# Quarter-column products of a modulation, issued by fours in place of pairs

## The chip, the cores and the metric

The kernel runs on one core of one Trainium2 chip. The metric is the device time of one execution in microseconds; of several runs the median is given. The profile is one execution taken by the hardware profiler; its rows are given in microseconds from the start of its span.

## What is computed

The reference is two transformer blocks behind each other, in float32, over 1024 tokens of width 1024. The first block modulates its input by a vector `c`, projects it to four mixers (an mLSTM, a gated spatial unit, a convolution and an S5 scan), projects back and runs a gated feed-forward layer. The second block normalises, projects, and runs attention, a state-space mixer and a linear recurrence. The part that the change touches is the modulation, which is one vector times a matrix:

```
mod = silu(c) @ w_mod[l] + b_mod[l]            # (1, 1024) @ (1024, 6144)
sh1, sc1, g1, sh2, sc2, g2 = split(mod, 6)
h = x * (1 + sc1) + sh1                        # needed first
x = layer_norm(ALPHA * x + g1 * (y @ w_out), ...)
x = layer_norm(ALPHA * x + g2 * swiglu(x * (1 + sc2) + sh2, ...), ...)
```

The first two sixths, `sh1` and `sc1`, are computed at the start of the kernel. The other four are the late modulation: 4096 columns, in eight parts of 512.

## The kernel before

The kernel is written as some forty Python generators, one for each stream of work (gates, an mLSTM pair, S5 batches, convolution taps, the projection, the out projection and so on). `weave` hands out their steps: every `yield t, wait` says how many microseconds of TensorE work the step is planned to take and how long the stream then waits, and at each moment the first stream of a fixed list (`STREAMS`) that is ready goes on. The late modulation is three entries: `mod_gate(0)` with parts 0 and 1 (the gate g1), `mod_cols` with parts 2 to 5 (sh2 and sc2), which follow each other in one stream, and `mod_gate(1)` with parts 6 and 7 (the gate g2), which starts when the out projection has its first accumulators. The program is then scheduled once more (`schedule_with_timeline_sim=True`), so that the order on an engine can differ from that of the code.

One part, `mod_part(n)` at line 1288, takes a PSUM bank `pm` (pmod in the trace) and an accumulator `acc` (macc). The 1024 rows of its weights are eight blocks of 128 rows by 512 columns, loaded by SyncE's queue two at a time into tiles `wm2` of 512 KB (wm in the trace), line 1301. Every block is one product, issued by `quarter` at line 440:

```
def quarter(p, kk, lhs, x):
    r0 = 32 * (kk % 4)
    pe.matmul(p[r0:r0 + 32, :], lhs, x, start=kk < 4, stop=kk >= 4)
```

The stationary side is one column of silu(c) repeated 32 times, so block `kk` fills 32 columns of TensorE and 32 partitions of the bank, the quarter `kk % 4`; blocks 4 to 7 are added to the quarters of blocks 0 to 3. ScalarE copies the bank to `acc` with the scale 1/32 (line 1311), and one more matmul sums the 128 partitions (line 1317) or turns them into a column (line 1325).

The loop over `q` runs five times. In turn it loads tile `q`, waits a planned 3.0, issues the two quarters of tile `q - 1`, frees that tile and counts 0.8 of TensorE work. So two tiles are held at most, and one load is always ahead of the pair that is issued. `spare` takes a free buffer from the list `ub` or else `u`; a freed buffer goes to the end of its list, and a load into it waits for whatever last read it. SyncE's queue also carries the other weights: `wpart` (line 219) loads 256 KB into one of three `raw` tiles, which ScalarE and VectorE or GpSimd split into a high and a low half (whi, wlo) for the other products (pz, psv, po, pf in the trace).

Of the kernel before, what the change touches and what calls it, by code (L numbers as in the profile page):

```python
# [75 lines left out]
def tile_block(ctx: ExitStack, tc: tile.TileContext, A, out):  # L76
    nc = tc.nc
# [32 lines left out]
    def ub(name, shape=None, dt=F32):  # L110
        return C["ub"].get(name, shape, dt)

    def f512(name):
        return C["f"].get(name)

    def bank(name, shape=None):
        return C["ps"].get(name, shape)

    def spare(name, shape=None, dt=F32, order=("u", "ub")):
        while not any(C[k].free for k in order):  # L120
            yield 0.0, 0.7
        k = order[0] if C[order[0]].free else order[1]
        return C[k].get(name, shape or (128, 1024), dt)

    def free(*ts):
        for t in ts:
            if isinstance(t, (list, tuple)):
                free(*t)
            else:
                next(c for c in C.values() if t.name in c.used).put(t)  # L130

    def need(**n):
        while any(len(C[k].free) < x for k, x in n.items()):
            yield 0.0, 0.7
# [56 lines left out]
    def col(name, i=0, n=1):  # L191
        return cols[:, COL0[name] + i:COL0[name] + i + n]
# [12 lines left out]
    def half(x, hf):  # L205
        return x[:, hf * 512:(hf + 1) * 512]
# [211 lines left out]
    cs = const.tile([128, 23, 2], F32, name="cs")  # L418
# [7 lines left out]
    wms = {}  # L426
# [13 lines left out]
# [4 lines that stand above are left out]
    def mod_part(st):  # L444
        pmt = bank("pmt", (128, 8, 2))
        for n in range(2):
            pm = bank("pmod")
            for q in range(4):
                x = wms[st + 2 * n, q]
                for k in range(2):  # L450
                    quarter(pm, 2 * q + k, cs[:, 2 * q + k:2 * q + k + 16, :].rearrange("p a b -> p (a b)"), x[:, k, :])
                free(x)
                yield 0.8, 0.0
            row = f512("modrow")
            v.tensor_copy(row[:], pm[:])
            free(pm)
            for c in range(4):
                pe.matmul(pmt[:, 4 * n + c, :], row[:, c * 128:(c + 1) * 128], fold[:], start=True, stop=True)
            free(row)
            yield 0.8, 0.0  # L460
        a, b = slice(4 * st, 4 * st + 4), slice(8 + 4 * st, 12 + 4 * st)
        bias = lambda r: col("b_mod", r.start, 4).unsqueeze(2).to_broadcast([128, 4, 2])
        v.tensor_tensor(modA[:, a, :], pmt[:, 0:4, :], bias(a), op=ALU.add)
        v.scalar_tensor_tensor(modA[:, b, :], pmt[:, 4:8, :], 1.0, bias(b), op0=ALU.add, op1=ALU.add)
        free(pmt)
# [77 lines left out]
    def mod_rest():  # L543
        while "A" not in state:
            yield 0.0, 0.7
        mod_load(1)
        ctx_load(1)
        state.add("L")
        while "h0" not in state:
            yield 0.0, 0.7  # L550
        yield from mod_part(1)
        ctx_split(1)
        state.add("h1")
# [30 lines left out]
    def start():  # L584
        if SCF:
            load_scols()
        mod_load(0)
        ctx_load(0)
        if not SCF:
            load_scols()  # L590
        state.add("T")
        yield 0.0, 8.0
        yield from mod_part(0)
        ctx_split(0)
        state.add("h0")
# [692 lines left out]
    def mod_part(n):  # L1288
        which = {0: 0, 3: 1}.get(n // 2)
        if which is not None and n % 2 == 0:  # L1290
            yield from need(ub=1)
            grow_[which] = ub(f"g{which}b", (128, 1024))
            nc.gpsimd.dma_start(grow_[which][:], A["g_b"][which:which + 1, :].to_broadcast([128, 1024]))
        yield from need(f=1, ps=1)
        acc = f512("macc")
        pm = bank("pmod")
        wms = []
        for q in range(5):
            if q < 4:
                wm = yield from spare("wm2", (128, 2, 512), order=("ub", "u"))  # L1300
                nc.sync.dma_start(wm[:], A["w_mod"][4 + n, :, 2 * q:2 * q + 2, :])
                wms.append(wm)
                yield 0.0, 3.0
            if q:
                wm = wms[q - 1]
                for k in range(2):
                    kk = 2 * (q - 1) + k
                    quarter(pm, kk, cs[:, kk, 0:1].to_broadcast([128, 32]), wm[:, k, :])
                free(wm)
                yield 0.8, 0.0  # L1310
        s.activation(acc[:], pm[:], AF.Copy, scale=1.0 / 32)
        free(pm)
        yield 0.0, 3.0
        yield from need(ps=1)
        if which is not None:
            p = bank("pmr")
            pe.matmul(p[:], ones[:], acc[:], start=True, stop=True)
            x = half(grow_[which], n % 2)
            v.tensor_tensor(x, x, p[:], op=ALU.add)
            if n % 2:  # L1320
                done.add(f"g{which}")
        else:
            p = bank("pmb", (128, 4, 2))
            for j in range(4):
                pe.matmul(p[:, j, :], acc[:, j * 128:(j + 1) * 128], ones[:, 0:2], start=True, stop=True)
            o = 4 * (n - 2)
            v.tensor_tensor(modB[:, o:o + 4], p[:, :, 0], col("b_mod", 24 + o, 4), op=ALU.add)
        free(p, acc)
        yield 1.0, 0.0

    def mod_cols():
        for n in (2, 3, 4, 5):
            yield from mod_part(n)
        sc2 = small("sc2", [128, 8], bufs=1)
        v.tensor_scalar(sc2[:], modB[:, 8:16], 1.0, None, op0=ALU.add)
        v.tensor_tensor(ln1c[:, 0], col("ln1_w", 0, 8), sc2[:], op=ALU.mult)
        v.tensor_tensor(ln1c[:, 1], col("ln1_b", 0, 8), sc2[:], op=ALU.mult)
        v.tensor_tensor(ln1c[:, 1], ln1c[:, 1], modB[:, 0:8], op=ALU.add)
        done.add("mod")
# [1265 lines left out]
```

## Time and profile before

| | us |
|---|---|
| median of 3 runs | 2351.17 |
| lowest and highest of the runs | 2348.05, 2354.90 |
| the profiled execution, its time | 2351.56 |
| its span, first to last instruction | 2349.8 |
| TensorE busy in the span | 2209.2 |

The mean granted clock of TensorE over the span is 0.969 of full speed. Busy times count instructions that run, not those that wait. The ends of matrix multiplications are modelled, and those that follow each other overlap in the rows, so the duration of one is longer than the step to the next.

### The profile page before, as it was taken

To read this page: it belongs to the slowest core of one execution; us is meant where nothing else is said; L and a number is where in the kernel's file an instruction comes from. 1 tells how busy PE (TensorE), PEld (TensorE's weight loads), DVE (VectorE), ACT (ScalarE), POOL (GpSimd) and SP (SyncE) were. 2 spreads that over 40 slices of the span, in tenths; PEclk is the share of its full clock that TensorE was granted. 3 is DMA by queue.
4 is the path that set the end of the run, shared out by engine and by line. 5 is a ranking of instruction groups with operands and counts; after the bars stand their busy time and mean duration, and the time that the engine had idled before them with its cause. 6 is when DMAs were issued, how large, how long until landed. Compare 5 with 4: busy or idle time off the path is not lost.

```text
span 2349.8 us, 29871 instructions
## 1 busy us (share of the span) xinstructions
PE 2209.2 (94%) x11002; PEld 1743.7 (74%) x11002; DVE 1209.7 (51%) x2192; ACT 815.1 (35%) x1497; POOL 926.2 (39%) x806
## 2 busy tenths in 40 slices
PE   5998879797999999999999999999999999989998
PEld 2787657575778888888888877687777777767877
DVE  8689744886881202112121497666544667575011
ACT  2423222443352111111212244344422455575322
POOL 4465534837654123232323445122563331022543
PEclk7999989798999999999999999999999999999999
DMA  7311444444322111111111334243576443332564
GB/s 275 97 49 50 141 148 139 138 146 149 91 69 75 47 52 45 50 41 58 45 59 54 99 117 146 87 154 105 159 211 178 166 162 130 103 112 94 148 194 141
DMA packets 161971, 265.87 MB, mean 113 GB/s; under 512 B 16409, under 2 KB 67481, under 8 KB 161825
## 3 DMA queue, kind: packets, MB, share of 16 engines
q1 hardware_dynamic: 127440, 219.21, 29.6%
q10 hardware_dynamic: 32112, 36.99, 4.6%
q0 software_dynamic: 2272, 7.77, 0.9%
q8 instruction: 86, 1.41, 0.3%
q14 instruction: 61, 0.49, 0.1%
HBM read 210.12 MB, written 52.74 MB: 112 GB/s over the span
## 4 chain that ended last, share of the span: by engine, by line
PE 66%; DVE 15%; DMA 7%; issue 4%; ACT 4%; POOL 4%; SPq 1%; ACTq 0%; POOLq 0%; DVEq 0%
PE pf L253 6%; PE pf L251 6%; PE pf L255 6%; PE pz L251 6%; PE pz L253 6%; PE pz L255 6%; PE pg L238 3%; PE pg L239 3%; PE pg L240 3%; PE pfo L238 2%; PE pfo L239 2%; PE pfo L240 2%; PE pO L2359 2%; DVE cv L809 1%; POOL wlo L212 1%
## 5 line engine op out<-in xcount | busy, mean ns | idle before, releaser
L212 POOL TENSOR_TENSOR wlo<-raw,whi 128x512 fp32r<-128x512 f32 (+1 forms) x285 | 394.8, 1388 | 877.4 <-ACT whi L215 857.9
L215 ACT ACTIVATE whi<-raw 128x512 fp32r<-128x512 f32 (+1 forms) x432 | 267.4, 622 | 992.0 <-PE pf L253 293.4
L212 DVE TENSOR_TENSOR wlo<-raw,whi 128x512 fp32r<-128x512 f32 (+1 forms) x147 | 114.8, 781 | 364.6 <-ACT whi L215 364.1
L255 PE MATMUL pf<-h,wlo 128*128 128x512 f32 x704 | 230.8, 391 | 3.9 <-POOL wlo L212 2.3
L253 PE MATMUL pf<-h,whi 128*128 128x512 f32 x704 | 231.3, 391 | 0.0
L251 PE MATMUL pf<-h,whi 128*128 128x512 f32 x704 | 231.2, 391 | 0.1
L251 PE MATMUL pz<-u,whi 128*128 128x512 f32 x512 | 171.2, 404 | 1.4 <-DVE sptmp L1794 0.6
L253 PE MATMUL pz<-u,whi 128*128 128x512 f32 x512 | 166.2, 394 | 0.0
L255 PE MATMUL pz<-u,wlo 128*128 128x512 f32 x512 | 165.8, 395 | 0.0
L255 PEld LDWEIGHTS pf<-h,wlo 128*128 128x128 f32 x704 | 132.1, 188 | 34.7 <-POOL wlo L212 3.7
L251 PEld LDWEIGHTS pf<-h,whi 128*128 128x128 f32 x704 | 132.1, 188 | 29.3 <-ACT whi L215 0.5
L253 PEld LDWEIGHTS pf<-h,whi 128*128 128x128 f32 x704 | 132.1, 188 | 29.2
L239 PE MATMUL pg<-wlo,act 128*128 128x512 f32 x352 | 138.3, 393 | 0.7 <-DVE wlo L212 0.5
L238 PE MATMUL pg<-whi,act 128*128 128x512 f32 x352 | 137.2, 393 | 1.2 <-ACT whi L215 1.2
L240 PE MATMUL pg<-whi,act 128*128 128x512 f32 x352 | 137.0, 392 | 0.0
L251 PEld LDWEIGHTS pz<-u,whi 128*128 128x128 f32 x512 | 95.9, 189 | 26.0 <-issue 3.0
L253 PEld LDWEIGHTS pz<-u,whi 128*128 128x128 f32 x512 | 96.3, 188 | 22.9 <-issue 1.4
L255 PEld LDWEIGHTS pz<-u,wlo 128*128 128x128 f32 x512 | 96.3, 188 | 22.0 <-issue 0.7
L1579 DVE TENSOR_TENSOR x<-x,pg 128x512 f32<-128x512 f32 x80 | 53.7, 685 | 109.5 <-PE pg L240 109.3
L239 PE MATMUL pfo<-wlo,mix 128*128 128x512 f32 x256 | 100.7, 394 | 1.7 <-POOL wlo L212 1.7
L1552 DVE TENSOR_TENSOR a<-a,pf 128x512 f32<-128x512 f32 x44 | 28.6, 683 | 140.7 <-PE pf L255 140.7
L240 PE MATMUL pfo<-whi,mix 128*128 128x512 f32 x256 | 100.4, 393 | 0.0
(628 smaller groups left out, 4810.7 us busy)
## 6 DMA issues: line engine op xcount, KB each, us to landing
raw<-in_w_ffn_in_dram SPq DMA_DIRECT2D x108, 256.0 KB
wm<-in_w_mod_dram SPq DMA_DIRECT2D x48, 512.0 KB
raw<-in_w_out_dram SPq DMA_DIRECT2D x96, 256.0 KB
raw<-in_w2f_dram SPq DMA_DIRECT2D x66, 256.0 KB
raw<-in_w_ffn_out_dram SPq DMA_DIRECT2D x56, 256.0 KB
raw<-in_w2q_dram SPq DMA_DIRECT2D x48, 256.0 KB
raw<-in_w_in_dram SPq DMA_DIRECT2D x36, 256.0 KB
mraw<-y2d SPq DMA_DIRECT2D x32, 256.0 KB
```

Source lines behind the costliest of these rows:

```text
L212: (v if dve else g).tensor_tensor(lo, full, hi, op=ALU.subtract)
L215: s.activation(hi, full, AF.Copy)
L238: pe.matmul(p, lh, rh, start=start, stop=False)
L239: pe.matmul(p, lh, rl, start=False, stop=False)
L240: pe.matmul(p, ll, rh, start=False, stop=stop)
L251: pe.matmul(p, wh, xh[k], start=k == 0, stop=False)
L253: pe.matmul(p, wh, xl[k], start=False, stop=False)
L255: pe.matmul(p, wl, xh[k], start=False, stop=k == kt - 1)
L809: v.scalar_tensor_tensor(a3, *tap(k), a3, op0=ALU.mult, op1=ALU.add)
L1552: v.tensor_tensor(a_[:], a_[:], pair[1][hf][:], op=ALU.mult)
L1579: v.tensor_tensor(x, x, p[t][:], op=ALU.add)
L2359: pe.matmul(pO[64 * x:64 * x + 64, b, :], va[:, jb, 64 * x:64 * x + 64], PT[2 * hp + x, ib][:, jb, :], start=jb == 0, stop=jb == ib)
```

## The change

`mod_part` no longer pipelines loads against pairs. It runs two rounds. Each round takes two tiles, issues both loads, waits a planned 5.0, issues the four quarters of the two tiles behind each other, frees both tiles and counts 1.0 of TensorE work. The products, their operands and the loads are the same.

```
-        wms = []
-        for q in range(5):
-            if q < 4:
-                wm = yield from spare("wm2", (128, 2, 512), order=("ub", "u"))
-                nc.sync.dma_start(wm[:], A["w_mod"][4 + n, :, 2 * q:2 * q + 2, :])
-                wms.append(wm)
-                yield 0.0, 3.0
-            if q:
-                wm = wms[q - 1]
-                for k in range(2):
-                    kk = 2 * (q - 1) + k
-                    quarter(pm, kk, cs[:, kk, 0:1].to_broadcast([128, 32]), wm[:, k, :])
-                free(wm)
-                yield 0.8, 0.0
+        for q0 in (0, 2):
+            wms = []
+            for q in (q0, q0 + 1):
+                wms.append((yield from spare("wm2", (128, 2, 512), order=("ub", "u"))))
+                nc.sync.dma_start(wms[-1][:], A["w_mod"][4 + n, :, 2 * q:2 * q + 2, :])
+            yield 0.0, 5.0
+            for k in range(4):
+                kk = 2 * q0 + k
+                quarter(pm, kk, cs[:, kk, 0:1].to_broadcast([128, 32]), wms[k // 2][:, k % 2, :])
+            free(wms)
+            yield 1.0, 0.0
```

## Rows read from the trace of the kernel before

**Rows 1.** The head of the page: span, and busy time of each engine.
```profile
span 2349.8 us, 29871 instructions
PE 2209.2 (94%) x11002; PEld 1743.7 (74%) x11002; DVE 1209.7 (51%) x2192; ACT 815.1 (35%) x1497; POOL 926.2 (39%) x806
```

**Rows 2.** Busy by stage: length; PE, PEld, DVE, ACT, POOL; clock, DMA share, GB/s.
```profile
255.00:345.00 90.00, 69.79 (x398) 52.24 (x397) 43.21 (x86) 21.68 (x41) 41.73 (x46) 0.89 0.53 164
345.00:445.00 100.00, 93.50 (x535) 68.26 (x533) 64.11 (x132) 38.59 (x79) 61.74 (x59) 0.95 0.53 169
445.00:540.00 95.00, 79.20 (x456) 63.41 (x454) 78.09 (x207) 37.21 (x93) 52.58 (x73) 0.88 0.36 120
540.00:665.00 125.00, 111.32 (x458) 81.56 (x459) 97.49 (x149) 46.51 (x84) 72.94 (x54) 0.90 0.33 102
665.00:900.00 235.00, 231.17 (x1023) 188.76 (x1022) 65.35 (x91) 65.36 (x121) 90.48 (x63) 1.00 0.20 61
```

**Rows 3.** Waits of TensorE, 255 to 445 us: total us, times, longest.
```profile
PE pmod L442 <- DMA wm<-in_w_mod_dram: 7.0, 3, 4.2
```

**Rows 4.** TensorE's timeline, line 442: start, length, count, [idle before, what ended it].
```profile
287.37 1.06 PE L442 MATMUL pmod<-wm,cs 128*32 128x512 f32 x8
294.71 1.94 PE L442 MATMUL pmod<-wm,cs 128*32 128x512 f32 x8 [2.23 <-DMA wm<-in_w_mod_dram]
318.59 1.93 PE L442 MATMUL pmod<-wm,cs 128*32 128x512 f32 x8 [4.23 <-DMA wm<-in_w_mod_dram]
...
367.55 1.05 PE L442 MATMUL pmod<-wm,cs 128*32 128x512 f32 x4
372.72 1.05 PE L442 MATMUL pmod<-wm,cs 128*32 128x512 f32 x4
377.99 1.06 PE L442 MATMUL pmod<-wm,cs 128*32 128x512 f32 x8
...
560.19 1.92 PE L442 MATMUL pmod<-wm,cs 128*32 128x512 f32 x16
624.14 1.04 PE L442 MATMUL pmod<-wm,cs 128*32 128x512 f32 x2
627.14 1.04 PE L442 MATMUL pmod<-wm,cs 128*32 128x512 f32 x2
...
638.48 1.07 PE L442 MATMUL pmod<-wm,cs 128*32 128x512 f32 x8
```

**Rows 5.** Busy time in two short stretches, columns as in the second group.
```profile
287.30:288.50 1.20, 1.20 (x10) 0.27 (x10) 0.00 (x0) 0.74 (x2) 1.03 (x1) 1.00 0.27 101
294.70:296.70 2.00, 1.99 (x9) 0.33 (x9) 0.00 (x0) 0.00 (x0) 0.00 (x0) 0.50 0.13 36
```

**Rows 6.** The chain of waits that ended last: start, length, what.
```profile
288.46 6.21 DMA wm<-in_w_mod_dram
...
311.74 6.81 DMA wm<-in_w_mod_dram
...
328.12 4.67 DMA wm<-in_w_mod_dram
...
367.62 0.98 PE pmod L442 x4
368.61 0.67 PE pz L251 x2
369.28 0.47 PE pz L253 x2
...
378.06 0.99 PE pmod L442 x8
...
637.50 3.33 DVE x L1529
```

**Rows 7.** The timeline of SyncE's queue: two issues of line 1301.
```profile
368.65 0.33 SPq L1301 DMA_DIRECT2D wm<-in_w_mod_dram  x1
...
379.08 0.33 SPq L1301 DMA_DIRECT2D wm<-in_w_mod_dram  x1
```

## The prediction, made before the change was run

> **What bounds the kernel now.** I read the head of the page first: the span, and how much of it TensorE is busy [rows 1]. 2209.2 of 2349.8 us leave 140.6 us of idle TensorE in the whole kernel. So a change pays either by taking work off TensorE where TensorE is never idle, or by shortening some of that idle time.
>
> The second view is busy time by stage, cut where the late modulation runs [rows 2]. The reader is to take from it the difference of the second column from the first. From 255 to 345 us TensorE is idle for 20.2 us, from 345 to 445 for 6.5, from 445 to 540 for 15.8 and from 540 to 665 for 13.7, together 56.2. From 665 to 900 it is 231.17 of 235, and there the feed-forward block needs nothing more than the end of this work. Five of the eight parts of the modulation and most of its loads lie in 255 to 445 us; the last two parts lie in 545 to 665 us.
>
> The third view is who waited for whom on TensorE in 255 to 445 us [rows 3]: the products of the modulation waited for their weight tiles three times, 7.0 us in all. The fourth is the timeline of TensorE, with the rows of line 442 alone [rows 4]. Each quarter-column product is two matrix multiplications in the trace, so a pair is x4, four together are x8. The chain of waits [rows 6] says which of these rows set the end, and the timeline of the SyncE queue [rows 7] says when a load could be issued.
>
> **The change, part by part.** *What already runs as four.* A part of the modulation has eight quarters, in the code four pairs. The trace doesn't show 32 pairs. In part 0 both rows are x8 (287.37 and 294.71 [rows 4]), and so are the two rows of part 1 (318.59, and one at 327.03 like that at 287.37) and of part 2 (at 332.84 and 341.63, the same). Parts 3, 4 and 5 are each a pair, a pair and a four: the three rows from 367.55 to 377.99 stand for all three parts. Part 6 is one row of x16, two fours. Part 7 is two single quarters (624.14, 627.14), one more pair at 635.51, and a four at 638.48. So of the 16 fours that the new code writes, 12 run as fours already, and only four are in pieces: three in two pieces, one in three. That is five separate passes to be saved, not sixteen.
>
> *What a piece costs.* A pair takes 1.05 us, a four 1.06, a single quarter 1.04 [rows 4]. The time doesn't depend on how many run side by side. In the chain a pair occupies 0.98 and a four 0.99 [rows 6]. There is something behind it too: the first two full-width products after the pair at 367.62 take 0.67 where the next two take 0.47, 0.20 more [rows 6]. So a separate piece costs 0.98 + 0.20 = 1.18 us; the floor, without the 0.20, is 0.98. I take 1.18, since both rows stand in one place on the chain.
>
> The Trainium skill, page TensorEngine Tiling, section Tiling Modes, says that changing the tiling mode drains TensorE. The 0.20 us agrees with it, and by that page fewer groups also mean fewer drains; without it the sum below would be 0.6 us smaller.
>
> *Where the five pieces lie.* Three are in parts 3, 4 and 5, in 345 to 445 us, two of them (parts 3 and 4) in the stretch up to 407 us where the chain runs along TensorE without a gap; I count all three: 3 x 1.18 = 3.5 us. The other two are in part 7. There the chain has left TensorE for VectorE (from 637.50 [rows 6]), so those 2 x 1.18 = 2.4 us are hidden by VectorE work and I count nothing; with that cover gone they add 2.4 us of gain.
>
> *The loads.* All 32 loads of 512 KB on SyncE's queue remain, in the same order and with the same two tiles held. What changes is when they may go. Now a load goes out when the pair ahead of it has freed its tile: 368.65 follows the pair at 367.55, which ends at 368.60, and 379.08 follows the four that ends at 379.05 [rows 4, 7]. The tile is used two steps later, and a step was 372.72 - 367.55 = 5.17 us. After the change two loads go out together when a four has freed both tiles, and both are wanted one step later, which the code plans as 5.0 us. The planner's step of before, 3.0 + 0.8 = 3.8, took 5.17 us in this stretch, so 5.0 should take 5.0 x 5.17 / 3.8 = 6.8 us. What must fit in there: a pair of loads issued together at 328.12 landed 4.67 us later, a single one behind other traffic 6.21, one at the end of a burst of six 6.81 [rows 6]. So the lead, about 10 us now, shrinks to 6.8, just enough for the slowest of these rows. I count no new wait; its bounds are 0 and, with a lead of only the planned 5.0, 6.81 - 5.0 = 1.81 us for each group. Behind a waiting product stands all of TensorE's queue, in this stretch the projection (pz) and the mLSTM products, which need nothing from these tiles.
>
> The Trainium skill, DMA: Bandwidth & Descriptors, section Anatomy of one DMA, gives for the other issuing path 2.0 us and a term of bytes / 436e3; that would be an estimate of 4.4 us for 1 MB, near the 4.67, and by it the loads are always in time. The rows of 6.21 and 6.81 speak against relying on it.
>
> *The three waits of before* (7.0 us [rows 3]) are in parts 0, 1 and 2. Two of them brought the clock down: the four after a wait of 2.23 us took 1.94 us at a granted clock of 0.50 (1.2 GHz), where the four at 287.37 took 1.06 at 1.00 (2.4 GHz) [rows 4, 5]. That is 0.88 us more, twice. In these parts the products are fours already, and the loads that came late were held by tiles in use elsewhere, so I keep these waits: gain 0, with a bound of 7.0 + 2 x 0.88 = 8.8 us.
>
> *The planned times.* A part is planned as 4 x 0.8 + 1.0 of TensorE now and as 2 x 1.0 + 1.0 after, 1.2 less, 9.6 over eight parts; its planned waits are 4 x 3.0 against 2 x 5.0, 2.0 less. What the parts yield is not what the code after them waits for longest (the out projection also waits for the whole projection, the first normalisation for the out projection), so an earlier end of a part gains nothing by itself: 0. But the other streams are handed out in another order. The idle 56.2 us of [rows 2] are waits in such an order; I take no change and, as bounds, a fifth of it to either side, 11.2 us (an assumption of mine, not a row).
>
> *Sum.* 2351.56 us (the profiled execution, 1.76 more than its span and 0.4 above the median of the runs) - 3.5 = 2348.1. By the median, 2347.7. I say 2348.
>
> **The rivals.**
> *The loads come late.* Two loads at once, both wanted at once, one step ahead. For it: tiles are scarce, as each load waits for a pair [rows 7], and three waits exist already. Against it: the lead of 6.8. It decides when the lead falls below the landing time. If the six groups of parts 3 to 5 each wait 1.81 us and run at the lower clock, 6 x (1.81 + 0.88) = 16.1, less the 3.5 gained: 2351.6 + 12.6 = 2364. Slower.
>
> *The old waits go.* The halved number of steps lets the early loads go out in time. For it: the three waits came from tiles freed late, and fewer waits for tiles are on SyncE's queue. Gain 3.5 + 8.8 = 12.3: 2339. Against it: the tiles of the early parts belong to other streams, which the change doesn't touch.
>
> *Another order of the streams.* Either sign: 2348.1 - 11.2 = 2337, or 2348.1 + 11.2 = 2359. For it: the order on TensorE is already not that of the code (two quarters of one pair run 3 us apart at 624.14 and 627.14). Against it: 665 to 900 us is full of TensorE work whatever the order [rows 2].
>
> *The fours are not fours.* The scheduler parts them again, as it did that pair: gain 0, 2351.6.
>
> **How the numbers follow.** A measurement of this kernel tells 0.3%, 7 us, from no change. Chances: the forecast 0.34; fours that are not fours 0.08; old waits gone 0.19; loads late 0.15; another order 0.24, half to each side. So faster 0.19 + 0.12 = 0.31, same 0.34 + 0.08 = 0.42, slower 0.15 + 0.12 = 0.27. The likeliest case alone spans 2344 to 2355: the five pieces at 1.18 and one or two waits gone at the lower end, one or two late pairs of loads at the upper. Cases of both signs hold 0.58, so the range reaches to the ends of the rivals, 2337 to 2364.
>
> **What would show it.** Line 442 in x8 rows alone, 16 of them, each near 1.06 us (1.94 where the clock is down), and its busy time in 345 to 445 us down from nine pieces to six. The waits of those products for weight tiles near 7 us; over 15 us, and the first rival is right, below 2, and the second is. Loads in twos on SyncE's queue, landing in 4.7 to 6.8 us. TensorE's idle time in 255 to 665 us near 56 us: if it moved by 7 us or more without the waits on weight tiles, the order did it. Wrong would be the prediction if TensorE's busy time fell by 6 us or so while the span didn't follow, or if the span moved with line 442 unchanged.

## The result, and the profile after

The changed kernel takes 2374.4 us (median of 5 runs, 2371.1 to 2379.1), the kernel before 2351.2: a ratio of 1.010, 95% interval 1.0081 to 1.0119. It is slower by 1.0%, 23 us. The forecast was 2348 with a range of 2337 to 2364; the time lies 10 us above its end. The profiled execution took 2371.11 us. Lines of the kernel after the changed loop have moved up by three (L1317 of before is L1314).

The head of the page, to be set beside [rows 1]:

```profile
span 2369.4 us, 29876 instructions
PE 2218.7 (94%) x11002; PEld 1749.4 (74%) x11002; DVE 1206.1 (51%) x2192; ACT 815.3 (34%) x1498; POOL 924.3 (39%) x806
```

TensorE runs the same 11002 matrix multiplications. Busy time is up by 9.5 us and idle time (span less busy) from 140.6 to 150.7, 10.1 us. So about half of the 19.6 us of span is idle, and half is the same work done in more time.

Busy time by stage, at the same times as in [rows 2]:

```profile
255.00:345.00 90.00, 73.54 (x401) 57.36 (x400) 43.27 (x80) 24.91 (x49) 40.71 (x45) 0.85 0.38 118
345.00:445.00 100.00, 92.05 (x512) 64.64 (x510) 69.10 (x137) 38.23 (x74) 60.80 (x54) 0.97 0.61 195
445.00:540.00 95.00, 77.76 (x453) 62.43 (x452) 73.53 (x193) 34.66 (x90) 45.73 (x72) 0.87 0.28 94
540.00:665.00 125.00, 102.59 (x434) 75.00 (x433) 87.65 (x140) 43.00 (x80) 81.47 (x59) 0.92 0.37 122
665.00:900.00 235.00, 227.60 (x996) 184.94 (x995) 73.32 (x113) 64.97 (x120) 85.19 (x59) 0.99 0.20 62
```

The first four stages are now idle for 16.5, 8.0, 17.2 and 22.4 us, together 64.1 against 56.2. The stage that was to be full whatever the order, 665 to 900, is idle for 7.4 us in place of 3.8.

TensorE's timeline, the rows of line 442, which answer to [rows 4]:

```profile
288.06 1.06 PE L442 MATMUL pmod<-wm,cs 128*32 128x512 f32 x8
320.93 1.93 PE L442 MATMUL pmod<-wm,cs 128*32 128x512 f32 x8 [0.16 <-DMA wm<-in_w_mod_dram]
328.64 1.06 PE L442 MATMUL pmod<-wm,cs 128*32 128x512 f32 x8 [2.08 <-DMA wm<-in_w_mod_dram]
...
389.44 1.05 PE L442 MATMUL pmod<-wm,cs 128*32 128x512 f32 x4
391.55 1.05 PE L442 MATMUL pmod<-wm,cs 128*32 128x512 f32 x4
...
413.97 1.91 PE L442 MATMUL pmod<-wm,cs 128*32 128x512 f32 x12
422.79 1.05 PE L442 MATMUL pmod<-wm,cs 128*32 128x512 f32 x4
...
444.15 1.05 PE L442 MATMUL pmod<-wm,cs 128*32 128x512 f32 x4
445.55 1.05 PE L442 MATMUL pmod<-wm,cs 128*32 128x512 f32 x4
...
580.88 1.92 PE L442 MATMUL pmod<-wm,cs 128*32 128x512 f32 x16
```

Two things are to be seen. Although the code now hands out fours only, four of the 16 still come apart on TensorE (three are shown, at 389, at 414 with its last pair at 422, and at 444; one at 356 runs as one quarter and three). A pass is a group of at most four quarters side by side; there are 20 of them in place of 21. And part 0, whose two fours stood 7 us apart before (287.37 and 294.71 [rows 4]), now has 33 us between them, 288.06 and 320.93.

Line 442 alone, the sum over 255 to 700 us, first of the changed kernel and then of the kernel before (TensorE busy, its weight loads):

```profile
sum 445.00, PE 21.64 PEld 3.30; mean PE 7.21 PEld 1.10
```

```profile
sum 445.00, PE 23.76 PEld 3.35; mean PE 7.92 PEld 1.12
```

The products themselves became 2.1 us cheaper. TensorE's waits, 255 to 700 us:

```profile
PE phn L1023 <- POOL num L1016: 10.8, 2, 10.5
PE pkt L895 <- DVE modB L1324: 5.6, 1, 5.6
PE pf L255 <- DVE wlo L212: 3.7, 1, 3.7
...
PE pmod L442 <- DMA wm<-in_w_mod_dram: 2.2, 2, 2.1
```

The wait for weight tiles, 7.0 us in [rows 3], is 2.2 us. The long waits are of other streams: 10.5 us in front of the second half of the mLSTM output, 5.6 for a PSUM bank that a part of the modulation gives on. On GpSimd, a load of the gating unit's scale rows stood behind a product, since its tile had just been a weight tile of the modulation (timeline of GpSimd):

```profile
345.11 1.14 POOL L1061 DMA_DIRECT2D sw<-in_sgu_ln_dram  x2 [18.93 <-PE pmod L442]
```

Where the 19.6 us arise can be read from the first and last matmuls of each stage in TensorE's timeline. The out projection (po) starts 11.4 us later (509.4, 520.8), the feed-forward block (pf) 10.6 later (657.3, 667.9), its second product (pg) 14.7 later (777.3, 792.0); the last pf is 17.3 later and the end 19.6. So half is lost before 668 us, four us in the first feed-forward blocks, the rest behind it. That rest, 4.9 us, is within what single executions of one kernel differ by (2348.05 to 2354.90 before). And the later start of po is no price by itself: in E8 below po starts at 518.6, and the first pf comes at 656.7.

TensorE up to the first pf, and from there to the first pg, columns as in [rows 2]; first before, then after:

```profile
0.00:657.30 657.30, 554.93 (x2906) 424.47 (x2906) 485.21 (x899) 227.54 (x455) 350.20 (x364) 0.90 0.39 127
657.30:777.30 120.00, 116.09 (x514) 93.57 (x515) 50.43 (x75) 43.52 (x84) 57.32 (x38) 1.00 0.25 77
```

```profile
0.00:667.90 667.90, 559.92 (x2908) 427.55 (x2909) 485.48 (x895) 227.57 (x455) 352.37 (x364) 0.91 0.38 125
667.90:792.00 124.10, 116.70 (x514) 94.30 (x513) 50.54 (x78) 44.01 (x86) 56.69 (x38) 0.99 0.24 75
```

Up to the first pf TensorE has the same matrix multiplications to run (two more after the change, the sum over the partitions of part 7, pmr). It idles 5.6 us longer, and the same work takes 5.0 us more, though the mean granted clock is no lower. Why it takes more, these rows don't show.

### The profile page after: what moved, and what is told of

It reads as the page before. It is cut to its first block, busy times and chain, and to the rows that moved or that the text cites. A ratio compares the mean times of both kernels' runs of the same rounds, so it can differ in the third digit from the quotient of the medians.

```text
span 2369.4 us, 29876 instructions
## 1 busy us (share of the span) xinstructions
PE 2218.7 (94%) x11002; PEld 1749.4 (74%) x11002; DVE 1206.1 (51%) x2192; ACT 815.3 (34%) x1498; POOL 924.3 (39%) x806
## 4 chain that ended last, share of the span: by engine, by line
PE 66%; DVE 15%; DMA 7%; POOL 4%; issue 4%; ACT 3%; SPq 0%; ACTq 0%; DVEq 0%; POOLq 0%
PE pz L251 6%; PE pf L255 6%; PE pf L251 6%; PE pf L253 6%; PE pz L253 6%; PE pz L255 6%; PE pg L239 3%; PE pg L240 3%; PE pg L238 3%; DVE cv L809 2%; DMA raw<-in_w_out_dram 2%; POOL wlo L212 2%; PE pO L2356 2%; PE pfo L238 2%; PE pfo L239 2%
## 5 line engine op out<-in xcount | busy, mean ns | idle before, releaser
L253 PEld LDWEIGHTS pz<-u,whi 128*128 128x128 f32 x512 | 96.7, 189 | 22.8 <-issue 1.4
```

Source lines behind the costliest of these rows:

```text
L253: pe.matmul(p, wh, xl[k], start=False, stop=False)
```

## The experiments

Four theories. **A, the order:** the kernel's planner hands out work by the planned times of all streams and by free buffers; the new loop comes up at other moments and takes and frees its tiles two at a time, so other streams get other places, and that order is slower. **B, the products or their loads:** fours, or loads issued in twos, arrive late or hold up TensorE. **C, one wait:** GpSimd's 19 us behind the products delays the gating unit, and the rest follows. **D:** each new part costs a fixed few us.

Ratios are to the kernel before on the same chip, with 95% intervals.

**E1, fours at the old times.** The old loop with all its planned waits; only the products are put together.
```
-            if q:
+            if q in (1, 3):
                 (four products of tiles q - 1 and q)
-                free(wm)
+                free(wms[q - 1], wms[q])
+            if q:
                 yield 0.8, 0.0
```


> The quarters run by fours (blocks 0 to 3 once tiles 0 and 1 are loaded, blocks 4 to 7 once 2 and 3 are), but every planned time and hand-over of the loop of before stays, so that the other streams are handed out nearly as before; the second tile of a four has a planned lead of only 3.0. Theory A (the loss is the new order of the other streams, not the fours): within 7 us of before, 2344 to 2358. Theory B (both tiles of a four wanted at once is what costs, loads come late): at least as slow as the changed kernel, 2370 or more, with waits of line 442 on its tiles over 15 us. Theory C (one wait of GpSimd at the row load of the gated spatial unit): near before too if that 18.9 us wait is absent.

**E2, pairs with the new totals.** The old loop, `yield 0.0, 3.0` made 2.5 and `yield 0.8, 0.0` made 0.5.

> The pairs and the load one ahead of before stay; only the planned times change, 0.5 in place of 0.8 and 2.5 in place of 3.0, so that a part is planned with the totals of the changed kernel (3.0 of TensorE work, 10.0 of waits and the last 3.0). Theory A (order): the time moves by more than 7 us although the loop is the old one; to 2360 to 2385 if the smaller totals themselves give the bad order. Theory B (late loads for fours): 2351, within 7 us. Theory C: moves only if GpSimd's wait at the row load of the gated spatial unit appears (near 19 us).

**E3, the new loop with the old totals.** `yield 0.0, 5.0` made 6.0, `yield 1.0, 0.0` made 1.6.

> The changed kernel with a planned wait of 6.0 in place of 5.0 and 1.6 in place of 1.0 behind each four, so that a part is planned as long as before (15.2 us) with as much TensorE work (3.2). Theory A (order, through the planned totals): most of the 23 us comes back, 2345 to 2362. Theory B (late loads): one more microsecond of lead takes at most the 2.2 us that the products still wait for their tiles, so 2370 or more. Theory C: fast only if GpSimd's wait is gone.

**E4, the changed kernel without GpSimd's wait.**
```
-            nc.gpsimd.dma_start(lnwb[:, i, :], A["sgu_ln"]...
+            nc.sync.dma_start(lnwb[:, i, :], A["sgu_ln"]...
```


> The changed kernel, with the two row loads of the gated spatial unit issued by SyncE's queue in place of GpSimd's, so that GpSimd no longer stands 18.9 us behind the quarter products whose tile that unit takes over; SyncE waits there anyway. Theory C (this wait is the loss): 2351 to 2362, GpSimd's wait gone and TensorE's products of the gated spatial unit done by about 408 us in place of 424. Theory A (the order as a whole): little of it, 2368 to 2377. Theory B (late loads): no change, 2374.

Measured: E1 1.0008 (0.9996 to 1.0021), E2 1.0037 (1.0022 to 1.0051), E3 1.0093 (1.0070 to 1.0116), E4 1.0083 (1.0064 to 1.0102).

E1 answers B for the fours of the code: TensorE waits 1.1 us for their tiles, and they cost nothing measurable. On TensorE five of E1's fours are parted again, 22 passes in all, so E1 doesn't show what a saved pass is worth. E3 says that the smaller planned totals are not needed for the loss, E2 that pairs with the new totals lose a third of it. For E3, theory A had foretold 2345 to 2362 through the totals and B 2370 or more. It measured 2371.3, so that form of A falls; but TensorE waited only 2.0 us for weight tiles, so B's late loads are not the reason. In E4 the wait of 18.9 us is gone from GpSimd's list, but the long waits of TensorE stand as in the changed kernel:

```profile
PE phn L1023 <- POOL num L1016: 10.9, 2, 10.6
PE pu L1192 <- DVE modB L1324: 7.0, 1, 7.0
PE pf L255 <- DVE wlo L212: 3.7, 1, 3.7
```

So GpSimd's standing there accounts for at most some 0.2%, and the intervals of E4 and of the changed kernel overlap. The edit doesn't make the rows of the gating unit earlier, though. SyncE's queue (first line) issues them at 343.26 us, where GpSimd did at 345.11 in the changed kernel. The unit's products (second line) last until 421.2, 424.2 in the changed kernel and 407.6 before; theory C had foretold 408. So E4 doesn't test what late rows cost.

```profile
343.26 0.90 SPq L1061 DMA_DIRECT2D sw<-in_sgu_ln_dram  x2
L1084 PE MATMUL psg<-sw,vn x64: 272/273/324, 398.6 to 421.2; 128*64 128x128 f32 x64
```

**E5, E6, E7, the new loop in some parts alone**, the old one in the others: `if n in (0, 1)`, `(2, 3, 4, 5)`, `(6, 7)`.

> The new loop in parts 0 and 1 alone (the gate g1); parts 2 to 7 keep the old one. Theory A (the loss comes with the order of the other streams, set where the parts are handed out among the mLSTM, S5 and gated spatial streams): the loss belongs to one group of parts, most likely the first, since the gated spatial unit's wait and the second mLSTM pair come behind it: 2360 to 2376 here and GpSimd's wait at line 1061 present. Theory D (each part costs by itself, about 23 / 8 = 3 us, in the loads or the steps of the loop): 2351 + 6 = 2357.

> The new loop in parts 2 to 5 alone (shift and scale of the second half). Theory A: within 7 us of before (2344 to 2358) if the first group makes the loss, 2365 or more if this one does; not in between by four parts' worth. Theory D: 2351 + 12 = 2363.

> The new loop in parts 6 and 7 alone (the gate g2), which run when the out projection does. Theory A: within 7 us of before, 2344 to 2358, the mLSTM's second pair as early as before (its last transposes near 560 us). Theory D: 2351 + 6 = 2357.

**E8, another order without the change.** The kernel before, with the planned wait of an S5 batch `yield 0.0, 4.0` made 5.0.

> A control: the kernel before with one planned wait of another stream moved by one microsecond (5.0 in place of 4.0 in an S5 batch, behind its two products on GpSimd); no instruction is added, removed or changed. If the time of this kernel hangs on the order alone (theory A), such a step too should move it by several us, to either side: anywhere in 2344 to 2372. If only the loop of the modulation matters (theories B and D), 2351 within 3.

Measured: E5 1.0052 (1.0036 to 1.0068), E6 1.0032 (1.0021 to 1.0043), E7 1.0020 (1.0011 to 1.0030), E8 0.9991 (0.9978 to 1.0004). Per part that is 6.1, 1.9 and 2.4 us (ratio less 1, times 2351, by parts), so D, a fixed cost, falls. The three add up to 1.04%, near the 1.0% of the whole; E17 below shows that this sum is not to be trusted. Theory A, as it was written down for these runs, did not hold either: it put the loss in one group of parts and E6 not in between, where it lies. It also had E8 move by several us. E8's order did change (po starts 9.2 us later), so E8 shows that not every change of order costs.

In E7 TensorE's course is that of before up to the first pf (658.5 against 657.3 us). The time is lost in the first feed-forward blocks: first pf to first pg takes 126.4 us, before 120.0. The waits of TensorE there, first of E7 from 655 to 800 us, then of the kernel before from 657 to 800:

```profile
PE pf L255 <- DVE wlo L212: 5.1, 2, 3.6
PE pf L255 <- POOL wlo L212: 2.1, 1, 2.1
```

```profile
PE pf L255 <- POOL wlo L212: 2.3, 1, 2.3
PE pf L255 <- DVE wlo L212: 1.5, 1, 1.5
```

The changed kernel has 5.3 and 2.1 in the same two waits. From the first pf to the first pg in E7:

```profile
658.50:784.90 126.40, 119.17 (x514) 96.06 (x513) 50.55 (x78) 44.11 (x86) 55.95 (x38) 0.96 0.23 73
```

So the 6.4 us are 3.3 of idle time (7.2 in place of 3.9) and 3.1 for the same 514 matrix multiplications, at a mean granted clock of 0.96 in place of 1.00.

VectorE splits the weights and the inputs that TensorE waits for. In the first normalisation it also scales two rows and, with them, the residual. The second row is scaled at 615.71 us in E7 and at 634.30 before, since the last parts are done earlier.

**E9, E7 with the scaling held back.**
```
         yield from after("ffa")
+        yield 0.0, 13.0
```


> The new loop in parts 6 and 7 alone, and in the first normalisation a planned wait of 13.0 us between the end of its work on the first feed-forward input and its scaling of the residual (the page of the kernel with the new loop in parts 6 and 7 shows that scaling handed out some 19 us earlier than before). If the 5.2 us of that kernel come from the scaling standing on VectorE ahead of the splits that TensorE waits for (theory A, order of the streams), they go: the time from the first pf to the first pg falls from 126.4 back to about 120 us, and the ratio is 1.000 +- 0.001. If the new loop costs the same wherever it stands, or if the 5.2 us have another cause, the ratio stays at 1.002.

Measured: 1.0015 (1.0005 to 1.0025), first pf to first pg 125.5 us. The planned wait did move the scaling of the two rows on VectorE; they were at 571.84 and 615.71 in E7:

```profile
613.19 0.69 DVE L1540 TENSOR_SCALAR lw<-lw 128x1024 f32<-128x1024 f32 x1 [1.30 <-DMA lw<-in_ln_dram]
624.57 0.68 DVE L1540 TENSOR_SCALAR lb<-lb 128x1024 f32<-128x1024 f32 x1
```

But the residual was not held back. VectorE scales the first of its four tiles 23.5 us ahead of the first pf, in E9 as in E7 (631.48 and 655.0 us; 635.00 and 658.5). The third follows 23 us behind the first pf (677.65), in E7 24 (682.07), where before it was 18 (675.64 and 657.3). TensorE's two waits are 5.1 and 2.1 us again. So the row scaling is not the cause, and the scaling of the residual is not tested by E9. What delays VectorE in E7 stays open.

**E10 and E11, between E1 and E3.** E1 costs nothing and E3 0.9%, with the same planned totals. E10 is E3's loop with E1's yields: both tiles are taken and loaded together, but the wait is again in two steps and the hand-over in two, with the next two loads between. In E11 the second tile is taken early and loaded at the old time.
```
             (take both tiles, load both; E11: load the first)
+            yield 0.0, 3.0
+            if q0:
+                yield 0.8, 0.0
             (E11: load the second)
+            yield 0.0, 3.0
             (four products)
             free(wms)
+            yield 0.8, 0.0
+        yield 0.8, 0.0
```


> The loop with fours at the old planned times, but the two tiles of a four are taken and their loads issued together, at the time of the first of them; planned waits, products and hand-overs as in that loop. Against the kernel with fours at the old times (ratio 1.0008) only the second tile and its load are 3 planned us (3.8 in the second half) earlier. If taking both tiles at once is what costs (they are missing elsewhere, theory A by way of the buffers), the ratio is 1.007 to 1.012, near the 1.0093 of the new loop with the old totals. If the single step of hand-over (1.6 in place of 0.8 and 0.8) is what matters, the ratio is 1.000 to 1.002.

> As the run with both tiles taken and loaded at once, but the second tile is only taken early; its load is issued at the old planned time. If the buffer taken early is what costs, the ratio is that of the run with both loaded early (1.007 to 1.012). If it is the two transfers side by side (or the load's place in SyncE's queue), the ratio falls to 1.000 to 1.003.

**E12, E5 without GpSimd's wait**, by the same two lines as E4.

> The new loop in parts 0 and 1 alone, with the two loads of the gating unit's scale rows issued on SyncE's queue in place of GpSimd's. If the 12.4 us of the new loop in parts 0 and 1 come from GpSimd standing 19 us behind quarter products (theory C), the ratio falls from 1.0052 to 1.000 to 1.002. If it is the order of the streams (theory A), the wait goes, the projection still ends near 420 us, and the ratio stays at 1.004 or more.

Measured: E10 1.0001 (0.9991 to 1.0011), E11 0.9993 (0.9982 to 1.0003), E12 1.0053 (1.0038 to 1.0069). E10 and E11 say that neither taking both tiles early nor issuing both loads at once costs by itself; TensorE waits 1.8 us for weight tiles in E10. For the loads that is a weak test, as they seldom run as twos: on SyncE's queue 9 of the 32 go out within 1 us of the one ahead in E10, 9 in the changed kernel and 9 before, since a load also waits for whatever last read its tile. E12 against E5's 1.0052 says of C what E4 did: GpSimd's wait, 19.0 us in E5, is gone, and the time is the same; but the rows go out at 348.1 us, 346.6 in E5, so they are no earlier.

**E13 and E14, one of the two remaining differences each.** E13 has the single wait of 6.0 and the hand-over in two steps; E14 two waits of 3.0 and one hand-over of 1.6. **E15** is the changed kernel with `yield 0.0, 5.0` as two of 2.5.

> The new loop with the old planned totals, with the hand-over after a four again 0.8, next two loads, 0.8 (and 0.8 and 0.8 at the end), and the wait one of 6.0. If the single step of hand-over was what cost the 0.9%, the ratio falls to 1.000 +- 0.002; if the single wait was, it stays at 1.007 to 1.011. If it is neither alone but simply another order (theory A: every order has its own price), the ratio lies anywhere in 0.999 to 1.010, and not at one of these two values for this run and the other for the next.

> The new loop with the old planned totals, the wait of a four in two steps of 3.0 and the hand-over one of 1.6. If the single wait was what cost the 0.9%, the ratio falls to 1.000 +- 0.002, and parts 6 and 7 take as long between their column adds as before (some 45 us, where the new loop takes 20); if the single hand-over was, it stays at 1.007 to 1.011.

> The changed kernel with its planned wait of 5.0 in two steps of 2.5: the sum is the same, the stream comes up for hand-out once more for each four. If the number of waits decides (a low stream is held back at each), parts 6 and 7 stretch towards the old times and the ratio falls from 1.010 to about 1.008, by the 0.2% that these parts cost; if the number doesn't matter, it stays at 1.010.

**E16, the changed kernel with its tiles kept through a part.**
```
+        wms = []
         for q0 in (0, 2):
-            wms = []
             for q in (q0, q0 + 1):
-                wms.append((yield from spare("wm2", ...)))
-                nc.sync.dma_start(wms[-1][:], ...)
+                if not q0:
+                    wms.append((yield from spare("wm2", ...)))
+                nc.sync.dma_start(wms[q - q0][:], ...)
...
-            free(wms)
             yield 1.0, 0.0
+        free(wms)
```


> The changed kernel with both tiles kept from the first four of a part to the second (the next two loads go into the same tiles), in place of giving them up and asking again. Planned times as in the changed kernel. If the early parts cost because another stream takes the tiles between the two fours, part 0 is done in one go as before, and the ratio falls by the 0.5% that parts 0 and 1 cost, from 1.010 to about 1.005; if the order of the streams costs in any case, it stays within 0.2% of 1.010.

Measured: E13 1.0041 (1.0023 to 1.0058), E14 1.0082 (1.0065 to 1.0098), E15 1.0088 (1.0072 to 1.0103), E16 1.0041 (1.0026 to 1.0055). Taken out of E3, the single hand-over gains 0.5% (E13) and the single wait 0.1% (E14). Put into E10 (1.0001), the single wait costs 0.4% (E13) and the single hand-over 0.8% (E14). So each costs, and the two effects don't add; E13's second 0.8 also stands ahead of the wait, where E10 has it between the two waits. E15 was placed at 1.008 by one theory and 1.010 by the other, and its interval doesn't part them.

E16 does what it says: part 0 is done in one go again (TensorE's timeline), and 0.6% is gained against the changed kernel:

```profile
289.11 1.07 PE L442 MATMUL pmod<-wm,cs 128*32 128x512 f32 x8
295.12 1.56 PE L442 MATMUL pmod<-wm,cs 128*32 128x512 f32 x8
297.87 1.02 PE L1315 MATMUL pmr<-macc,ones 128*128 128x512 f32 x2
```

That looked like the cause: the tiles, freed in twos, go to another stream, and the second four of part 0 stands 33 us behind the first, until new ones are loaded. But E1 has the same hole and costs nothing:

```profile
287.85 1.06 PE L442 MATMUL pmod<-wm,cs 128*32 128x512 f32 x8
323.18 1.94 PE L442 MATMUL pmod<-wm,cs 128*32 128x512 f32 x8 [1.08 <-DMA wm<-in_w_mod_dram]
```

**E17 and E18, two tests of that.** E17 keeps the tiles in parts 0 to 5 and has the old loop in 6 and 7. E18 is E10 with the tiles kept.

> The new loop with both tiles kept through a part in parts 0 to 5, the old loop in parts 6 and 7. If the costs add, the 0.2% of parts 6 and 7 leave the 0.41% of the kernel with kept tiles: a ratio of 1.002, and the time from the first pf to the first pg back from 126 to 120 us. If the price belongs to the order as a whole (theory A in its wide form), it can't be foretold: 0.999 to 1.006.

> Fours, both tiles of a four loaded together, tiles kept through a part, planned times as before the change. If giving the tiles up costs by itself, this is faster than the kernel with both tiles early and given up (1.0001): 0.997 to 0.999. If that hole costs only together with the new planned times, 0.999 to 1.002.

Measured: E17 1.0065 (1.0049 to 1.0082), E18 1.0084 (1.0068 to 1.0101). Both narrow theories fail, and E17 lies just above even the 0.999 to 1.006 of the wide one. E17 takes the costly loop out of parts 6 and 7 and gets slower than E16 by 0.24%, where it should have gained 0.2% (the two intervals overlap, but 1.002 is well below E17's); first pf to first pg is back at 121.5 us as foretold, but the first pf comes at 669.3 in place of 658.3. E18 keeps the tiles at the old times and loses 0.8% against E10. Keeping them gains 0.6% with one set of planned times and costs 0.8% with the other. In E18 the rows of the gating unit go out at 316.1 us and its products last until 407.9, as before, so a loss of this size needs no late rows. E18's waits on TensorE, 255 to 675 us, are again others:

```profile
PE pmb L1327 <- ACT macc L1313: 9.0, 1, 9.0
PE pst L911 <- ACT sp L774: 8.0, 1, 8.0
```

All kernels in the order of the first pf, with the idle time of TensorE before it (both from TensorE's timeline of the one profiled execution, while the ratio is over all runs):

| kernel | first pf, us | idle before it, us | ratio |
|---|---|---|---|
| E10 both early | 653.7 | 95.4 | 1.0001 |
| E11 taken early | 654.5 | 94.9 | 0.9993 |
| E9 parts 6, 7, held | 655.0 | 103.9 | 1.0015 |
| E1 fours, old times | 655.3 | 96.7 | 1.0008 |
| E8 S5 wait alone | 656.7 | 103.6 | 0.9991 |
| before | 657.3 | 102.4 | 1 |
| E2 pairs, new totals | 657.6 | 102.5 | 1.0037 |
| E16 tiles kept | 658.3 | 100.7 | 1.0041 |
| E7 parts 6, 7 | 658.5 | 104.0 | 1.0020 |
| E6 parts 2 to 5 | 661.6 | 101.5 | 1.0032 |
| E13 split hand-over | 662.9 | 103.2 | 1.0041 |
| changed kernel | 667.9 | 108.0 | 1.0100 |
| E12 parts 0, 1, no GpSimd wait | 668.2 | 105.4 | 1.0053 |
| E17 kept, 0 to 5 | 669.3 | 104.4 | 1.0065 |
| E4 no GpSimd wait | 669.6 | 109.4 | 1.0083 |
| E5 parts 0, 1 | 669.8 | 104.6 | 1.0052 |
| E14 split wait | 670.4 | 104.4 | 1.0082 |
| E18 kept, old times | 673.4 | 115.6 | 1.0084 |
| E15 new, split wait | 674.7 | 114.0 | 1.0088 |
| E3 old totals | 677.2 | 115.6 | 1.0093 |

The ratio goes roughly with the start of the feed-forward block, and only in part with idle time: in E5 TensorE is idle 2.2 us more than before and the block starts 12.5 us later. TensorE runs the same 2906 matrix multiplications ahead of it in all kernels (2908 where the pmr of part 7 comes first), so the other 10.3 us are the same work taking longer.

Seven kernels lose a further 4 to 7 us between first pf and first pg: E2, E4, E7, E9, E15, E16 and the changed one take 124.1 to 126.8 us, with 7.2 to 7.4 idle. They are the seven in which the pmr of part 7 is done more than 30 us ahead of the first pf. In the other thirteen it is done 13 us ahead at most, and the stretch takes 119.4 to 122.6, with 2.6 to 5.1 idle. No run tests this by itself; E9 kept the early end.

None of the kernels is faster than before by more than can be measured.

## Why the prediction was wrong

**What failed** is the last term of the sum, "the planned times": the other streams "are handed out in another order", for which I took "no change" and, as bounds, a fifth of the idle 56.2 us, 11.2 us, an assumption without a row. It measured 23 us in the medians, or an estimated 25 if the 2.1 us that line 442 lost in busy time count as gained. The rival of that name stood at 0.24, half to each side, and ended at 2359; it had the right mechanism with the wrong size. Its bound failed twice over. It counted idle time between 255 and 665 us alone, which did grow by 7.9 us, within the bound. But idle time is not the whole price of an order: up to the first pf it grew by 5.6 us and the time of the same matrix multiplications by 5.0 (in E5 by 2.2 and 10.3). And the price reaches past 665: "full of TensorE work whatever the order" is refuted by 7.4 us idle in 665 to 900, 3.8 before.

**The separate pieces.** I counted 16 fours handed out together, so five passes saved; one was. The scheduler parted four of them again, so the rival to which I gave 0.08 was nearly the case. Line 442's busy time fell by 2.1 us all the same, of which a pass accounts for 1; the rest is in how many of the products ran at the lower clock. What a saved pass is worth on the span no run shows: on TensorE E1 has 22 passes and E10 has 21, no fewer than before. That the span moved with line 442 nearly unchanged is the second sign of being wrong that I wrote.

**The loads** brought no new wait, as I had it: the waits for weight tiles fell to 2.2 us. But the reason is not tested, since the loads did not go out in twos on the queue any more often than before. The rival of late loads, at 2364, is refuted. Two readings were wrong, with no term resting on the first: six, not five, of the eight parts lie in 255 to 445 us, and the load of 6.81 us [rows 6] was the second of six issues from 310.2 to 321.3 us, not the end of the burst.

**The old waits** I expected to stay, at 7.0 us; under the test that I wrote down (over 15, or below 2) 2.2 is nearest to their going. It gained nothing visible, since the time was lost elsewhere.

**The test of order** that I wrote, idle time in 255 to 665 us moving by 7 us or more without the waits on weight tiles, is met: it moved by 7.9, and without those waits (7.0 before, 2.2 after) by 12.7.

**What is shown and what is open.** Shown: E10, E13, E14 and E3 have the same products, loads and planned totals and differ in their yields alone, and they lie between 1.0001 and 1.0093. So the hand-out sets the price. Shown too: that neither the fours of the code (E1), nor both loads issued at once (E10), nor GpSimd's wait (E4, E12), nor the smaller totals alone (E3), nor the row scaling of the normalisation (E9) is the cause, and that the same edit changes sign with the planned times around it (E16 against the changed kernel, E18 against E10). That leaves theory A in its wide form: the moments at which this stream yields, takes tiles and frees them set the order of all the others, and the price belongs to the whole order. In this form it foretells neither size nor sign. Not shown: through which single displaced step most of the 23 us comes. The steps named on the way (the 10.5 us in front of phn, the late rows of the gating unit, the early end of part 7, the bank handed on at pkt) each appear in some slow kernels, and no run removed one of them and got its time back.

## What to carry to other kernels

In a kernel whose streams are interleaved by planned times, a local edit should be tried first with every yield, request and release left where it was (E1, 1.0008), since the same products with a changed hand-out cost 1%. Price a changed hand-out by a few neighbouring orders of the same kernel and not by a share of the idle time: the eighteen here lay between 0.999 and 1.009, effects found one at a time did not add, and an edit that gained in one order (kept tiles) lost in another.

## What the runs showed of the hardware

A DMA issue on GpSimd waits in that queue for the tile that it will fill: 18.9 us behind the quarter products, with GpSimd's other work behind it. That so long a wait cost nothing measurable when the issue went to SyncE's queue (E12, 1.0053 against 1.0052) I had not expected.

In two rows of the changed kernel the clock doesn't go with a product's own wait. The four at 320.93 us waited 0.16 us for its tile and took 1.93 us, at a granted clock of 0.50 (1.2 GHz); the four at 328.64 waited 2.08 us and took 1.06 us at 1.00 (2.4 GHz). The windows ahead of each and around each, columns as in [rows 5]:

```profile
316.00:320.90 4.90, 1.93 (x10) 1.23 (x9) 0.00 (x0) 3.62 (x5) 0.00 (x0) 0.85 0.55 192
320.90:322.90 2.00, 1.97 (x9) 0.31 (x9) 0.00 (x0) 1.13 (x2) 0.00 (x0) 0.50 0.41 92
322.90:328.60 5.70, 3.64 (x20) 2.46 (x20) 4.10 (x12) 1.19 (x2) 1.93 (x5) 0.99 0.69 259
328.60:329.70 1.10, 1.06 (x9) 0.25 (x9) 0.00 (x0) 0.00 (x0) 0.00 (x0) 1.00 0.41 156
```

What TensorE did ahead of them differs: 1.9 us of work in 4.9 before the slow one, 3.6 in 5.7 before the fast one. Which of that matters, these rows don't tell; that two of the old waits "brought the clock down", as the prediction has it, is not shown either.
